# Scoring the samples' cached keys in the even layer instead of in the attention stage

## The chip, the cores and the metric

One core of a Trainium2 chip. The time is device microseconds of one execution of the whole program. Engines: PE (TensorE matmul), PEld (its weight loads), DVE (VectorE), ACT (ScalarE), POOL (GpSimd) and SP (SyncE, which issues most DMAs). Arrays live in device memory (DRAM), working tiles in the on-chip buffer, matmul results in PSUM.

## The reference

One inference step of two layers. The even layer has HGRN2 heads (chunked gated linear attention) and forgetting-attention heads ("fox") side by side; the odd layer is GLA. A prompt of 2048 tokens is worked on together with samples: 8 sequences of 4 new tokens, each with 2048 past tokens in a paged cache. The change touches the samples' attention to that cache:

```
def fox_sample(q, k, v, log_f, k_pages, v_pages, logf_pages, page_table):
    ...
    k_past = k_pages[page_table].reshape(db, -1, H, dh)
    v_past = v_pages[page_table].reshape(db, -1, H, dh)
    lf_past = logf_pages[page_table].reshape(db, -1, H).astype(jnp.float32)
    ...
    suffix_past = (lax.cumsum(lf_past, axis=1, reverse=True) - lf_past).swapaxes(1, 2)
    logit_past = jnp.einsum('bthd,bshd->bhts', q, k_past).astype(jnp.float32) * scale \
        + cum_new[..., None] + suffix_past[:, :, None, :]
    ...
    p = jax.nn.softmax(jnp.concatenate([logit_past, logit_new], axis=-1), axis=-1).astype(v.dtype)
    return jnp.einsum('bhts,bshd->bthd', p[..., :P], v_past) + jnp.einsum('bhts,bshd->bthd', p[..., P:], v)
```

There are 8 sequences x 16 pages; a page holds 128 keys x 4 heads x 128 elements in float32, 256 KB. The keys are 32 MB, the values 32 MB.

## The kernel before

The program has four stretches: the even layer's first half of the prompt, its second half (with the samples), the attention stage (`phase_fox`), and the odd layer. A half of the even layer is 16 dense **units** (weights of one projection against all tokens of the half, three float16 matmuls for each product, lines 630 to 632), numbered 0 to 15 and 16 to 31 and given by `staged`; each unit is yielded in pieces, n = 0, 1, 2, 3 and so on. Beside them run four heads of linear attention (`lin_attn`, lines 700 to 930: gl, gd, qA, kA, o_A and the like), woven in by `mux` in proportion to costs written in the code. Between pieces `staged` calls `ahead(pool, u, n)`, which works on the cached keys, and `beside`, which measures the scale of 20 "later" weight units (a load `lr`, four DVE reduces at line 307, a small matmul `spr`); all 20 are in the second half.

**Keys.** One tile is four pages (1 MB): one page column j of four sequences (group g = 0 or 1), 32 tiles in all. A loaded tile (`kp` or `pgcache_fox_k`) is turned by four DVE transposes (`turn_block`, line 1535) into `kt`, keys along the free dimension. 20 of the tiles (`AHEAD`, units 4 to 13 and 19 to 28) are loaded at piece 1 (line 1531), turned at piece 3 and piece 0 of the next unit, and stored at line 1551 to the DRAM array `kT`. They use buffers "lr" in the first half and "wr" in the second, where raw weights are loaded too.

**Attention.** `fox_prompt` (scores `s`, softmax through `mx`, `nm` and `L`, transposes `pt`, their float16 parts `th` and `tl`, products with the values `fo`) and `fox_sample` are generators; `until` steps the one that is behind by the costs they yield, scaled by `FOX_P` and `FOX_S`. `fox_sample` first makes `qz` (queries masked for a sequence, line 1630). Then for each tile n it fetches the turned tile `ktd` from `kT` (line 1597), or loads four pages and turns them into `kts`, and gives the 16 matmuls of the tile before (`score`, line 1697) through `strips`: four heads side by side on 32 columns of PE each, into a PSUM bank `sc` of four pages:

```
            return lambda: nc.tensor.matmul(sc[32 * h : 32 * h + 32, j % 4 * P : (j % 4 + 1) * P], qz[:, g, 4 * h + x],
                                            kt[:, 4 * h + x], start=(j % 4, g, x) == (0, 0, 0), stop=False,
```

After four page columns, 16 matmuls of `sel` with `suf` (line 1726) add the forget values' suffix sums of `past()`, and one DVE instruction (line 1729) adds a zero column, takes the maximum and writes the bank to `pr`. After four banks come the exponential, the transposes of `pr` to `pT`, and for each of 32 value tiles a fetch (`pgcache_fox_v`) and four matmuls (`pv`, line 1777).

Three things order this. `issue_after` places an instruction behind a named one in the recorded order. `KAHEAD` and `PKLAG` keep the turning and the scores within a distance of the prompt's work. `page_regs` reads page numbers into SP's registers, so page loads go through SP's queue in order.

Of the kernel before, what the change touches and what calls it, by code (L numbers as in the profile page):

```python
# [8 lines left out]
F32 = mybir.dt.float32  # L9
# [10 lines left out]
P = 128  # L20
# [14 lines left out]
SC_C = 1350.0  # L35
# [4 lines left out]
EWR = 3  # L40
# [10 lines left out]
AHEAD = (*range(4, 14), *range(19, 29))  # L51
PRE = len(AHEAD)
TURNED = [n for n in range(2 * 16) if (n + 1) * PRE // 32 > n * PRE // 32]
PAST = 3
VAHEAD = 3
KAHEAD = 6
PKLAG = 4
# [10 lines left out]
PV_C = 5860.0  # L68
# [60 lines left out]
class Kern:  # L129
# [6 lines left out]
    def consts(self):  # L136
# [31 lines left out]
        self.kT = dp.tile([PRE, P, 4 * 512], F32, name="kT")  # L168
# [465 lines left out]
    def proj_fm(self, pps, act, W, off, M, hf, evac, nm):  # L634
        for c0, n in self.segs(hf):
            ps = pps.tile([P, 512], F32, tag="pj", name=f"pf_{nm}{c0}")
            for k in range(KT):
                self.mm3(ps[:M, :n], [x[:, k, off : off + M] for x in W],
                         [x[:, k, c0 : c0 + n] for x in act], k == 0, k == KT - 1)
# [3 lines left out]
    def proj_tm(self, pps, act, W, hf, evac, nm, width=256, pairs=True, banks=("pj",)):  # L643
# [3 lines left out]
        for g in range(0, len(tl), per):  # L647
# [8 lines left out]
            for j, (c0, n) in enumerate(grp):  # L656
                for k in range(KT):
                    self.mm3(ps[:n, j], [x[:, k, c0 : c0 + n] for x in act],
                             [x[:, k, :width] for x in W], k == 0, k == KT - 1)
# [463 lines left out]
    def phase_even(self):  # L1123
# [4 lines left out]
        with pool("act", side="right") as ap, pool("w", side="right") as w0, pool("wl", side="right") as wp1, \  # L1128
                pool("wk") as wp0, pool("nrm") as n0, pool("stt") as sp, pool("ps", space=PSUM) as pp0:
            wpool = self.wpool = Pool(w0, {"w": 3, "wr": EWR, "rm": 2, "pow": 2, "lr": 2})  # L1130
            wp = Pool(wp0, {"c4": 7, "sam": 1, "v4": 3, "sg": 3, "pd": 1, "kt": 2, "y": EY, "xpad": 1, "vs": 3,
                            "ss": 2, "rs_t": 2, "rs_r": 2}, Pool(wp1, {"c2": EC2, "th": ETH}))
# [14 lines left out]
            def beside(x):  # L1147
                x -= 33
                for n in (1, 2):
                    if 0 <= x - 1 < len(self.later):  # L1150
                        self.later[x - 1][n]()
                if 0 <= x < len(self.later):
                    self.later[x][0]()

            self.later, self.kept = [], {}
# [4 lines left out]
            for hf in range(2):  # L1160
# [7 lines left out]
                def dense(a, b, hf=hf):  # L1168
                    return self.staged(us, 16 * hf + a, 16 * hf + b, beside)
# [33 lines left out]
                else:  # L1203
                    self.sx_odd = self.gain_scale(self.g_odd, pps, "pj", "o")
                    self.later = [self.later_unit(wpool, pps, w, cols, key, undo) for w, cols, key, undo in
                                  self.later_units()]
# [7 lines left out]
                drain(dense(2 - hf, 3))  # L1214
                drain(mux(lin(0), LIN_E[hf], dense(3, 5), 2 * cost))
# [35 lines left out]
            for n in range(2):  # L1251
                self.ahead(wpool, 32, n)
# [14 lines left out]
    def staged(self, us, a, b, beside=None):  # L1267
# [1021 lines left out]
```

## Time and profile before

| | |
|---|---|
| median of 3 runs | 2319.26 us (2313.12 to 2326.04) |
| profiled execution | 2321.78 us, its span 2320.1 us |
| mean granted clock of TensorE | 0.983 |
| even layer, attention, odd layer (about, in the trace) | 0 to 880, 880 to 1260, 1260 to 2320 us |
| stores and fetches of turned keys | 20 and 20, of 1024 KB |
| page loads of keys | 80 of 256 KB in the even layer, 48 in the attention |

In a row of grouped instructions or of the timeline, the line of the kernel, engine and operation come first, then output <- inputs, the shape, how often (x), the busy time and the mean of one in ns, and last the idle time of that engine ahead of them with what ended it. "PE s L630 <- DVE mx L1421: 16.8, 12, 7.5" reads: PE waited before the matmuls into s for DVE's instructions on mx, 16.8 us in all, 12 times, 7.5 us at the longest. PE's granted clock is a share of full speed.

### The profile page before, as it was taken

To read this page: it belongs to the slowest core of one execution; us is meant where nothing else is said; L and a number is where in the kernel's file an instruction comes from. 1 tells how busy PE (TensorE), PEld (TensorE's weight loads), DVE (VectorE), ACT (ScalarE), POOL (GpSimd) and SP (SyncE) were. 2 spreads that over 40 slices of the span, in tenths; PEclk is the share of its full clock that TensorE was granted. 3 is DMA by queue.
4 is the path that set the end of the run, shared out by engine and by line. 5 is a ranking of instruction groups with operands and counts; after the bars stand their busy time and mean duration, and the time that the engine had idled before them with its cause. 6 is when DMAs were issued, how large, how long until landed. Compare 5 with 4: busy or idle time off the path is not lost.

```text
span 2320.1 us, 58035 instructions
## 1 busy us (share of the span) xinstructions
PE 2206.3 (95%) x23316; PEld 1580.6 (68%) x23316; DVE 1399.2 (60%) x3138; ACT 991.6 (43%) x2200; POOL 727.1 (31%) x788
## 2 busy tenths in 40 slices
PE   7999999999999996889999999999999999999998
PEld 5677667864655684556446888677677666667887
DVE  7766567626555555768768445366665655547554
ACT  6433344221121223446566443555544545545343
POOL 2223334001111103434346245154452432323232
PEclk9999999999999998999999999999999999999999
DMA  6356665975766549997984969524224431115553
GB/s 203 121 163 187 192 194 188 284 177 172 224 197 183 169 136 271 250 264 271 277 265 142 311 196 262 126 75 146 73 92 97 126 94 58 47 58 165 169 188 151
DMA packets 365296, 403.87 MB, mean 174 GB/s; under 512 B 108529, under 2 KB 303410, under 8 KB 355810
## 3 DMA queue, kind: packets, MB, share of 16 engines
q1 hardware_dynamic: 362882, 393.54, 57.4%
q0 software_dynamic: 2144, 6.62, 0.8%
q8 instruction: 183, 3.00, 0.5%
q14 instruction: 87, 0.71, 0.1%
HBM read 265.77 MB, written 117.39 MB: 165 GB/s over the span
## 4 chain that ended last, share of the span: by engine, by line
PE 69%; DMA 10%; DVE 8%; ACT 4%; issue 4%; SPq 2%; POOL 2%; POOLq 0%; DVEq 0%; ACTq 0%
PE pt_o L630 4%; PE pt_o L631 4%; PE pt_o L632 4%; DMA pgcache_fox_k<-in_cache_fox_k 3%; PE pt_Cv L630 2%; PE pt_Cv L632 2%; PE pt_Cv L631 2%; PE pt L1457 2%; DMA ny<-in_x_prompt 1%; PE pv L1777 1%; PE gl_A L761 1%; PE o_C L914 1%; PE pt_Av L632 1%; PE pt_Av L630 1%; PE pt_Av L631 1%
## 5 line engine op out<-in xcount | busy, mean ns | idle before, releaser
L630 PE MATMUL pt_o<-w_o,act 128*128 128x256 f16 x1024 | 278.9, 273 | 1.3 <-ACT sg1C L687 1.3
L631 PE MATMUL pt_o<-w_o,act 128*128 128x256 f16 x1024 | 278.9, 273 | 0.0
L632 PE MATMUL pt_o<-w_o,act 128*128 128x256 f16 x1024 | 278.7, 273 | 0.0
L630 PEld LDWEIGHTS <-act 128*128 128x128 f16 x2304 | 226.6, 98 | 37.1 <-issue 3.7
L631 PEld LDWEIGHTS <-act 128*128 128x128 f16 x2304 | 226.7, 98 | 33.5 <-issue 4.8
L632 PEld LDWEIGHTS <-act 128*128 128x128 f16 x2304 | 226.6, 98 | 30.7 <-issue 2.2
L794 POOL TENSOR_TENSOR kA<-kA,fA 128x512 f32<-128x512 f32 (+1 forms) x56 | 76.8, 1372 | 338.8 <-PE gl_A L761 275.7
L1429 ACT ACTIVATE L<-L,nm,kc 128x512 f32<-128x512 f32 (+3 forms) x160 | 118.2, 741 | 75.1 <-DVE nm L1427 58.6
L630 PE MATMUL pt_Cv<-w_Cv,act 128*128 128x256 f16 (+1 forms) x512 | 141.4, 276 | 0.3 <-DMA act<-xs 0.3
L632 PE MATMUL pt_Cv<-w_Cv,act 128*128 128x256 f16 (+1 forms) x512 | 141.3, 276 | 0.0
L631 PE MATMUL pt_Cv<-w_Cv,act 128*128 128x256 f16 (+1 forms) x512 | 141.3, 276 | 0.0
L1437 POOL TENSOR_SCALAR L<-L,nm 128x512 f32<-128x512 f32 (+3 forms) x160 | 100.0, 639 | 130.7 <-DVE nm L1433 65.4
L794 POOL TENSOR_TENSOR kC<-kC,fC 128x512 f32<-128x512 f32 (+1 forms) x56 | 81.9, 1463 | 136.3 <-PE gl_C L761 91.4
L1464 ACT ACTIVATE th<-pt 128x512 f16<-128x512 f32 (+3 forms) x159 | 81.0, 527 | 94.6 <-PE pt L1457 92.7
L1465 DVE TENSOR_TENSOR tl<-pt,th 128x512 f16<-128x512 f32 (+3 forms) x159 | 94.5, 605 | 13.0 <-ACT th L1464 11.2
L1457 PE MATMUL pt<-ident,L 128*128 128x128 f32 x544 | 89.6, 280 | 9.4 <-DVE tl L1465 7.5
L1457 PEld LDWEIGHTS pt<-ident,L 128*128 128x128 f32 x544 | 65.5, 143 | 36.1 <-DVE tl L1465 12.8
L793 DVE TENSOR_TENSOR qC<-qC,fC 128x512 f32<-128x512 f32 (+1 forms) x56 | 72.9, 1301 | 21.1 <-PE gl_C L761 21.1
L1977 ACT ACTIVATE vC<-pt_Cv,kc 128x512 f32<-128x512 f32 (+1 forms) x40 | 23.9, 598 | 133.9 <-PE pt_Cv L632 133.9
L630 PE MATMUL s<-k,q 128*128 128x512 f16 (+3 forms) x160 | 57.4, 359 | 20.0 <-DVE mx L1421 16.8
L630 PE MATMUL pt_Bv<-w_Bv,act 128*128 128x260 f16 (+1 forms) x256 | 70.4, 275 | 3.5 <-DVE kc L279 2.3
L630 PE MATMUL pt_Bk<-w_Bk,act 128*128 128x256 f16 x256 | 71.3, 278 | 0.3 <-DVE Bvs L1075 0.3
(961 smaller groups left out, 6473.9 us busy)
## 6 DMA issues: line engine op xcount, KB each, us to landing
pgcache_fox_v<-in_cache_fox_v SPq DMA_DIRECT2D x128, 256.0 KB, 4.5
kp<-in_cache_fox_k SPq DMA_DIRECT2D x80, 256.0 KB, 5.3
kT<-kt SPq DMA_DIRECT2D x20, 1024.0 KB, 5.0
ktd<-kT SPq DMA_DIRECT2D x20, 1024.0 KB, 14.1
yr<-yT SPq DMA_DIRECT2D x16, 1024.0 KB, 7.3
pgcache_fox_k<-in_cache_fox_k SPq DMA_DIRECT2D x48, 256.0 KB, 13.3
x1d<-xo SPq DMA_DIRECT2D x44, 256.0 KB, 4.2
wr_o<-in_w_out_even SPq DMA_DIRECT2D x32, 256.0 KB, 5.5
```

What stands on the lines that cost most here:

```text
L630: nc.tensor.matmul(ps, lh[0], rh[0], start=first, stop=False)
L631: nc.tensor.matmul(ps, lh[0], rh[1], start=False, stop=False)
L632: return nc.tensor.matmul(ps, lh[1], rh[0], start=False, stop=last)
L761: nc.tensor.matmul(ps[o : o + M, ch], k[:, ch * P + r : ch * P + r + M], rhs[:, :, 1], start=True, stop=True, tile_position=(0, o))
L793: nc.vector.tensor_tensor(xv[:, :, 1], xv[:, :, 1], t0.to_broadcast([P, nb, w]), ALU.mult)
L794: nc.gpsimd.tensor_tensor(kv[:, :, 0], kv[:, :, 0], t1.to_broadcast([P, nb, w]), ALU.mult)
L1429: self.last_exp = nc.scalar.activation(lt[:, :w], lt[:, :w], AF.Exp, bias=nm[:, 0:1], scale=ib, accum_out=nm[:, 2 + j : 3 + j])
L1437: nc.gpsimd.tensor_scalar(lt[:, :w], lt[:, :w], nm[:, 1:2], 2.0**14, ALU.mult, ALU.mult)
L1457: nc.tensor.transpose(pt[:, w : w + P], rows[b][s // 4][0][:, (s % 4) * P : (s % 4 + 1) * P], self.ident)
L1464: nc.scalar.activation(th[:, a:w], pt[:, a:w], AF.Copy),
L1465: nc.vector.tensor_tensor(tl[:, a:w], pt[:, a:w], th[:, a:w], ALU.subtract)))
L1977: r = nc.scalar.activation(v[h][:, g : g + cnt], ps[:, :, :256], AF.Copy, scale=c)
```

## The change

All 32 key tiles are handled in the even layer, at positions t = 4 x unit + piece that the list `KEYS` gives: four at 52, 56, 60 and 64, then one at every second t from 68 to 122. A tile is loaded at t, turned at t + 2 and t + 3, and its 16 matmuls are given at t + 4, behind the last dense matmul given so far, into a bank of "gr", the two banks that the linear attention's gl and gd use. For g = 0 ACT copies the result to `scs`, for g = 1 DVE adds its result to that, and at t + 5 the 64 KB are stored to the DRAM array `scd`. `kT` goes. `qz` is made at unit 12 (`queries`). Ten later units move into the first half. The attention fetches the scores as one 1 MB load into `pr`, and adds them where it took the maximum; its yields are longer in places, so that the sample's work is spread over the prompt's in another way. Buffers: "wr" 4 in place of 3, "lr" 1 in place of 2, "rm" and "pow" 3 in place of 2.

```
-EWR = 3
+EWR = 4
-AHEAD = (*range(4, 14), *range(19, 29))
+KEYS = (*range(4 * 13, 4 * 17, 4), *range(4 * 17, 4 * 31, 2))
+LATER = (*range(4, 14), *range(17, 27))
-PV_C = 5860.0
+PV_C = 10080.0
...
-        self.kT = dp.tile([PRE, P, 4 * 512], F32, name="kT")
+        self.scd = dp.tile([P, T], F32, name="scd")
...
-            wpool = self.wpool = Pool(w0, {"w": 3, "wr": EWR, "rm": 2, "pow": 2, "lr": 2})
+            wpool = self.wpool = Pool(w0, {"w": 3, "wr": EWR, "rm": 3, "pow": 3, "lr": 1})
...
+            def beside(j, n):
+                if n == 0 and j - 1 in LATER:
+                    for step in self.later[LATER.index(j - 1)][1:]:
+                        step()
+                if n == 1 and j in LATER:
+                    self.later[LATER.index(j)][0]()
...
+                if beside and n < 4:
+                    self.ahead(self.wpool, pps, 4 * j + n)
+                    beside(j, n)
...
-                with ExitStack() as st:
-                    if len(self.pks) > PKLAG:
-                        st.enter_context(self.tc.issue_after(self.pks[-1 - PKLAG].ins))
-                    self.last_pe = self.mm3(ps[:, :w], q, [x[:, :w] for x in K[h, j]], True, True)
+                self.last_pe = self.mm3(ps[:, :w], q, [x[:, :w] for x in K[h, j]], True, True)
...
+    def queries(self, wp, s):
+        nc = self.nc
+        if s == 0:
+            self.q4 = wp.tile([P, 512], F32, tag="c2", name="q4").rearrange("p (x t) -> p x t", t=TS)
...
+            return
+        with self.tc.issue_after(self.last_dve.ins):
+            for hp in range(2):
+                x = slice(8 * hp, 8 * hp + 8)
+                for g in range(2):
+                    nc.vector.scalar_tensor_tensor(self.qz[:, g, x], self.q4[:, x], self.fsc["q", hp][1],
+                                                   self.bm[:, g : g + 1].to_broadcast([P, 8, TS]), ALU.mult, ALU.mult)
+
+    def ahead(self, pool, pps, t):
+        nc, wp = self.nc, self.few
+        if t in (4 * 12, 4 * 12 + 2):
+            self.queries(wp, t % 4)
+
+        def turns(x):
+            with self.tc.issue_after(self.last_dve.ins):
+                self.made += [self.turn_block(self.kt_ahead, self.kp_ahead, y) for y in (x, x + 1)]
+
+        if t - 5 in KEYS and KEYS.index(t - 5) % 2:
+            j = KEYS.index(t - 5) // 2
+            nc.sync.dma_start(self.scd[:, j * P : (j + 1) * P], self.scs)
+        if t - 4 in KEYS:
+            j, g = divmod(KEYS.index(t - 4), 2)
+            ps = pps.tile([P, 512], F32, tag="gr", name=f"ks{j}{g}")[:, :P]
+            kt, made = self.kts.pop(0)
+
+            def score(x, h):
+                return lambda: nc.tensor.matmul(ps[32 * h : 32 * h + 32], self.qz[:, g, 4 * h + x], kt[:, 4 * h + x],
+                                                start=x == 0, stop=x == 3, tile_position=(0, 32 * h))
+
+            with self.tc.issue_after(self.last_mm.ins):
+                self.strips([score(x, h) for x in range(4) for h in range(NH)], made)
+            if g == 0:
+                self.scs = wp.tile([P, P], F32, tag="scs", name=f"scs{j}")
+                nc.scalar.activation(self.scs, ps, AF.Copy)
+            else:
+                nc.vector.tensor_tensor(self.scs, ps, self.scs, ALU.add)
+        if t - 3 in KEYS:
+            turns(2)
+            self.kts.append((self.kt_ahead, self.made))
+        if t - 2 in KEYS:
+            n = KEYS.index(t - 2)
+            self.kt_ahead, self.made = pool.tile([P, NH * 4, P], F32, tag="wr", name=f"kt{n}"), []
+            self.kp_ahead = self.kps.pop(0)
+            turns(0)
+        if t in KEYS:
+            n = KEYS.index(t)
+            kp = pool.tile([P, 4, 512], F32, tag="wr", name=f"kp{n}")
             with self.tc.issue_after(self.last_sp.ins):
-                regs = self.page_regs(TURNED[m] % 2, TURNED[m] // 2)
+                regs = self.page_regs(n % 2, n // 2)
                 for x in range(4):
-                    self.page_load(self.kp_ahead, "cache_fox_k", regs[x], x)
...
+                    self.page_load(kp, "cache_fox_k", regs[x], x)
+            self.kps.append(kp)
...
+        nc.sync.dma_start(pr[:, :T], self.scd)
+        yield 8000
...
+        for c in range(4):
+            sc = pps.tile([P, 512], F32, tag="sc", name=f"sc{c}")
+            for jj in range(4):
+                for h in range(NH):
+                    nc.tensor.matmul(sc[32 * h : 32 * h + 32, jj * P : (jj + 1) * P],
+                                     env["sel"][:, 4 * c + jj].rearrange("p b t -> p (b t)"), env["suf"][:, h],
+                                     start=jj == 0, stop=jj == 3, tile_position=(0, 32 * h))
+            part = pr[:, c * 512 : (c + 1) * 512]
+            nc.vector.tensor_tensor_reduce(part, sc, part, 1.0, -3e38 if c == 0 else mx[:, c - 1 : c], ALU.add, ALU.max,
+                                           mx[:, c : c + 1])
+            yield 3000
```

In the rows of order that follow, a number behind a name tells its buffer; ISA is the prompt's add with a running maximum, and its read of that maximum.

On DVE at the attention's start, in the first head's second group, before:

```order
L1535 STREAM_TRANSPOSE kts00_11760<-pgcache_fox_k00_11755 128x16x32
L1421 ISA L070_11769,mx07_11764<-s070_11765,cb0_11493 128x512
L1421 ISA mx07_11764 128x1
L1535 STREAM_TRANSPOSE kts00_11760<-pgcache_fox_k00_11755 128x16x32 x3
L1480 SCALAR_TENSOR_TENSOR fy000_11791<-fo00_11566,kc_67,fsg00_11496 128x512
L1432 TENSOR_REDUCE nm06_11675<-nm06_11675 128x1
L1421 ISA L071_11776,mx07_11764<-s071_11772,cb0_11493,mx07_11764 128x384
L1421 ISA mx07_11764 128x1
L1535 STREAM_TRANSPOSE kts01_11948<-pgcache_fox_k01_11943 128x16x32 x3
```

and after:

```order
L1418 TENSOR_SCALAR nm06_12846<-mx06_12832,kc_67 128x1
L1412 ISA L070_12879,mx07_12874<-s070_12875,cb0_12664 128x512
L1412 ISA mx07_12874 128x1
L1456 TENSOR_TENSOR tl0003_12824<-pt0003_12821,th0003_12823 128x128
L1412 ISA L071_12885,mx07_12874<-s071_12881,cb0_12664,mx07_12874 128x384
L1412 ISA mx07_12874 128x1
L1412 ISA L071_12885,mx07_12874<-s071_12881,cm07_12872,mx07_12874 128x128
L1412 ISA mx07_12874 128x1
L1471 SCALAR_TENSOR_TENSOR fy000_12899<-fo00_12737,kc_67,fsg00_12667 128x512
```

The transposes between the parts of row block 7's maximum are gone, and with them the waits for pages that stood ahead of it.

On PE in the second half, within the unit Bk0 (output pt_Bk100), before:

```order
L632 MATMUL pt_Bk100_10249<-w_Bk01_9635,act_121 128x256
L630 LDWEIGHTS act_121
L630 MATMUL pt_Bk100_10249<-w_Bk01_9635,act_121 128x256
L631 LDWEIGHTS act_121
L631 MATMUL pt_Bk100_10249<-w_Bk01_9635,act_121 128x256
```

and after:

```order
L627 MATMUL pt_Bk100_11031<-w_Bk01_10249,act_121 128x256
L1571 MATMUL ks110_10647<-kt22_10446,qz_4856 32x128 x16
L625 LDWEIGHTS act_121
L625 MATMUL pt_Bk100_11031<-w_Bk01_10249,act_121 128x256
L626 LDWEIGHTS act_121
L626 MATMUL pt_Bk100_11031<-w_Bk01_10249,act_121 128x256
```

The 16 score matmuls of key tile 22 now stand between two of the unit's dense matmuls, and those behind them pass only when they have.

On DVE in the second half, where the linear attention of head 1 ends (y_A111) and that of head 2 begins (qA12), before:

```order
L744 SCALAR_TENSOR_TENSOR y_A1110_8952<-py_A1110_8947,g_hgrn_781,sg11_6896 128x512
L1535 STREAM_TRANSPOSE kt14_8900<-kp14_8751 128x16x32
L1535 STREAM_TRANSPOSE kt15_9129<-kp15_9014 128x16x32 x3
L296 TENSOR_REDUCE pow_Cg3_9141<-spr_Cg3_9139 128x1
L1535 STREAM_TRANSPOSE kt15_9129<-kp15_9014 128x16x32
L307 TENSOR_REDUCE rm_o11_9550<-lr_o11_9335 128x1 x4
```

and after:

```order
L739 SCALAR_TENSOR_TENSOR y_A1110_9436<-py_A1110_9431,g_hgrn_781,sg11_6921 128x512
L1526 STREAM_TRANSPOSE kt17_9489<-kp17_9328 128x16x32 x4
L291 TENSOR_REDUCE pow_o11_9837<-spr_o11_9835 128x1
L280 TENSOR_SCALAR pow_o11_9837<-pow_o11_9837 128x1
L281 TENSOR_SCALAR kc_67<-pow_o11_9837 128x1
L1526 STREAM_TRANSPOSE kt18_9626<-kp18_9492 128x16x32 x4
L282 RECIPROCAL kc_67<-kc_67 128x1
L1580 TENSOR_TENSOR scs8_9487<-ks81_9608,scs8_9487 128x128
L1526 STREAM_TRANSPOSE kt19_9784<-kp19_9629 128x16x32 x4
L702 COPY_PREDICATED dg_882<-mdiag_861,gd_A12_9700 128x256
```

Twelve transposes of three key tiles now stand together where five stood, with the four reduces of a later weight unit gone from there.

More of the change, by code (lines that the diff above doesn't have):

```diff
@@ L34 @@
 S0 = 12000.0
-SC_C = 1350.0
 Z_C = 4000.0
@@ L1214, in phase_even @@
                 drain(dense(2 - hf, 3))
+                if hf == 0:
+                    self.sx_odd = self.gain_scale(self.g_odd, pps, "pj", "o")
+                    self.later = [self.later_unit(wpool, pps, w, cols, key, undo) for w, cols, key, undo in
+                                  self.later_units()]
                 drain(mux(lin(0), LIN_E[hf], dense(3, 5), 2 * cost))
@@ L1250, in phase_even @@
             drain(last)
-            for n in range(2):
-                self.ahead(wpool, 32, n)
+            for t in range(4 * 32, 4 * 32 + 2):
+                self.ahead(wpool, pps, t)
     def later_units(self):
@@ L1589, in pages @@
             return t, r
-        def turned(n):
-            kt = fs.tile([P, NH * 4, P], F32, tag="pg", name=f"ktd{n}")
-            with ExitStack() as st:
-                if len(asked) < 8:
-                    st.enter_context(self.tc.issue_after(first_v.ins))
-                d = nc.sync.dma_start(kt.rearrange("p a s -> p (a s)"), self.kT[n])
-            asked.extend([d] * 4)
-            kts.append((kt, [d]))
         yield S0
-        marks, steps, first_v = [], [], self.last_vload
+        marks, first_v = [], self.last_vload
         qs = one([P, NH, TS], "qs")
@@ L1690, in past @@
                                  start=False, stop=True)
[L1691 removed]
+                yield 2000
             suf = one([P, NH, P], "suf")
             nc.vector.tensor_copy(suf, psf)
[L1694 to L1699 removed]
@@ L1701, in fox_sample @@
-        kts, ins = [], []
-        sc = None
-        for n in range(2 * NPG + 1):
-            if n < 2 * NPG:
-                j, g = n // 2, n % 2
-                if n in TURNED:
-                    turned(TURNED.index(n))
-                    yield 4 * SC_C
-                else:
-                    yield from turn(pages("cache_fox_k", g, j)[0], g, j)
-            if n == PAST:
-                yield from past()
-                self.y_bounds(pps)
-            if n == 0:
-                continue
-            j, g = (n - 1) // 2, (n - 1) % 2
-            c = j // 4
-            if (j % 4, g) == (0, 0):
-                sc = pps.tile([P, 512], F32, tag="sc", name=f"sc{c}")
-            kt, made = kts.pop(0)
-            self.pks.append(self.strips([score(h, g, j, x, kt, sc) for x in range(4) for h in range(NH)],
-                                        made))
-            if (j % 4, g) == (3, 1):
-                for jj in range(4):
-                    for h in range(NH):
-                        nc.tensor.matmul(sc[32 * h : 32 * h + 32, jj * P : (jj + 1) * P],
-                                         env["sel"][:, 4 * c + jj].rearrange("p b t -> p (b t)"), env["suf"][:, h],
-                                         start=False, stop=jj == 3, tile_position=(0, 32 * h))
-                nc.vector.tensor_tensor_reduce(pr[:, c * 512 : (c + 1) * 512], sc, env["zcol"].to_broadcast([P, 512]), 1.0,
-                                               -3e38 if c == 0 else mx[:, c - 1 : c], ALU.add, ALU.max,
-                                               mx[:, c : c + 1])
-                yield 1200
@@ new lines, in past @@
+            env.update(suf=suf, sel=sel, mnew=mnew, ntb=ntb)
+        yield from past()
+        self.y_bounds(pps)
+        for c in range(4):
[9 more added lines that the diff above has]
+            yield 3000
```

99 lines of the change are left out of this document (20 added, 79 removed).

## The prediction

> **What bounds the kernel now.** I read the page first, then busy time by stage, then the waits of the attention stage.
>
> ```profile
> span 2320.1 us, 58035 instructions
> PE 2206.3 (95%) x23316; PEld 1580.6 (68%) x23316; DVE 1399.2 (60%) x3138; ACT 991.6 (43%) x2200; POOL 727.1 (31%) x788
> PE   7999999999999996889999999999999999999998
> PE 69%; DMA 10%; DVE 8%; ACT 4%; issue 4%; SPq 2%; POOL 2%; POOLq 0%; DVEq 0%; ACTq 0%
> ```
>
> PE is busy 95% of the span and nearly everywhere, except in three slices just past the middle (6, 8, 8). Moving work of PE's from one full stage to another gains nothing; only PE's idle time and its slow clock can go. The busy table by stage says where they are (columns: length, busy time and count of PE, PEld, DVE, ACT, POOL, then PE's granted clock, the DMA engines' share, GB/s). The rows are the even layer's first half, its second half, the attention's first 200 us, the attention's rest, and the odd layer:
>
> ```profile
> 0.00:440.00 440.00, 411.23 (x4681) 302.99 (x4682) 298.90 (x678) 186.15 (x425) 132.24 (x138) 0.99 0.61 184
> 440.00:880.00 440.00, 428.25 (x4454) 288.55 (x4451) 234.27 (x533) 92.06 (x231) 53.52 (x56) 0.99 0.65 190
> 880.00:1080.00 200.00, 162.45 (x1822) 104.29 (x1822) 139.52 (x463) 91.01 (x221) 68.75 (x132) 0.91 1.04 268
> 1080.00:1260.00 180.00, 171.54 (x1137) 91.67 (x1138) 137.56 (x449) 112.31 (x267) 84.72 (x138) 0.99 0.70 222
> 1260.00:2320.00 1060.00, 1032.83 (x11228) 793.12 (x11225) 588.94 (x1018) 510.06 (x1057) 387.90 (x326) 0.99 0.45 138
> ```
>
> The attention's first 200 us lose 200 − 162.45 = 37.6 us idle, and (1 − 0.91) × 200 = 18 us to the clock, while the DMA engines are full (1.04). It is the stretch in which the cached keys are fetched, turned and scored. Its rest, with the values in place of the keys, loses 8.5 us idle and 1% of clock. The even layer's second half, which is to take the work over, has PE busy 428 of 440 us: no room on PE, much on DVE (234 of 440).
>
> What PE and DVE waited for in the attention (total, times, longest), and one such wait by the clock:
>
> ```profile
> DVE kts L1535 <- DMA pgcache_fox_k<-in_cache_fox_k: 26.3, 7, 11.0
> PE s L630 <- DVE mx L1421: 16.8, 12, 7.5
> PE pt L1457 <- DVE tl L1465: 7.5, 7, 3.7
> PE sc L1697 <- DMA ktd<-kT: 6.1, 2, 4.6
> PE fo L631 <- DVE tl L1465: 5.4, 7, 2.3
> PE s L630 <- DMA vn<-vs: 3.0, 1, 3.0
> 910.05 1.90 DVE L1535 STREAM_TRANSPOSE kts<-pgcache_fox_k 128x512 f32<-128x512 f32 x3 [7.41 <-DMA pgcache_fox_k<-in_cache_fox_k]
> 912.31 0.61 PE L630 MATMUL s<-k,q 128*128 128x512 f16 x1 [7.54 <-DVE mx L1421]
> ```
>
> By name PE waits for the prompt's own softmax (mx, tl). The last two rows show what stands behind that name: at 910.05 DVE had stood 7.41 us before a transpose whose page had not landed, the prompt's maximum was queued behind it, and PE's 7.54 us ended 2.3 us later. A wait of DVE for a page becomes a wait of PE for mx.
>
> **What goes from the attention.** First the scores' matmuls:
>
> ```profile
> L1697 PE MATMUL sc<-ktd,qz x640: 272/273/422, 903.2 to 1063.3; 128*32 128x128 f32 x160
> L1697 PE MATMUL sc<-kts,qz x384: 272/273/423, 901.5 to 1061.5; 128*32 128x128 f32 x192
> 942.31 1.08 PE L1697 MATMUL sc<-ktd,qz 128*32 128x128 f32 x32
> 943.32 0.49 PE L1688 MATMUL psf<-stri,lfTs 128*128 128x128 f32 x2
> 1051.62 2.76 PE sc L1697 x96
> ```
>
> 640 + 384 = 1024 records are 32 tiles of 32 records (16 program matmuls, two passes each). They overlap, so a tile's price is the time until the next matmul starts: 943.32 − 942.31 = 1.01 us for a tile that stands alone, 2.76 / 3 = 0.92 us in threes (from the chain of waits). Middle 0.97: 32 × 0.97 = **−31 us**. The 16 sel matmuls of each bank stay.
>
> Then the waits. Of 37.6 + 18 = 55.6 us I let 16 stay: what remains of the stretch, about 200 − 31 − 40 = 129 us, loses at the rate of the attention's rest, 8.5 / 180 idle and 1% clock, 7.4 us; the rest is a wait that has nothing to do with keys (vn, 3.0) and the start's own softmax chain. So **−40 us**. Bounds: −50 (5 or 6 stay) and −17 (rival B). What speaks for the high end: the queue that made DVE wait empties. These fetches leave it:
>
> ```profile
> ktd<-kT SPq DMA_DIRECT2D x20, 1024.0 KB, 14.1
> kT<-kt SPq DMA_DIRECT2D x20, 1024.0 KB, 5.0
> pgcache_fox_k<-in_cache_fox_k SPq DMA_DIRECT2D x48, 256.0 KB, 13.3
> ```
>
> 20 MB of turned keys and 12 MB of raw ones no longer arrive during attention, and 20 MB are no longer stored before it. What comes instead is one fetch of the 1 MB of scores, and 16 stores of 64 KB in the even layer, under 2 MB together. The values' 32 MB now start near the attention's beginning, since the sample's yields are longer, so its traffic is spread rather than front-loaded.
>
> **What the even layer takes over.** The same 512 matmuls, now in a dense stream that leaves no gap: **+31 us** (29 at 0.92, 32 at 1.01). They stand alone there, 16 between dense ones, so the upper price is the nearer, but the price in threes is the lower end.
>
> [...]
>
> DVE's part is in the next rows (groups of the first half's and then the second half's transposes, a reduce of the second half, and a 128x128 copy of the attention):
>
> ```profile
> L1535 DVE STREAM_TRANSPOSE kt<-kp 128x512 f32<-128x512 f32 x40 | 25.8, 684 | 9.2 <-DMA kp<-in_cache_fox_k 9.2
> L1535 DVE STREAM_TRANSPOSE kt<-kp 128x512 f32<-128x512 f32 x40 | 25.9, 685 | 9.8 <-DMA kp<-in_cache_fox_k 9.7
> L307 DVE TENSOR_REDUCE rm_o<-lr_o 128x1 f32<-128x512 f32 x32 | 20.0, 674 | 3.7 <-DMA lr_o<-in_w_out_even 3.7
> L1755 DVE COPY pT<-ppt 128x128 f32<-128x128 f32 x16 | 3.4, 277 | 0.3 <-PE ppt L1752 0.3
> ```
>
> Three of the 32 tiles are turned in the first half and 29 in the second. The first half loses 28 of 40 transposes (19 us) and gains 10 later units of 4 reduces (27 us): DVE 299 to about 307 of 440. The second half gains 76 transposes (52 us), loses 40 reduces (27 us), and gains 16 adds of 0.28 us (by the copy's row): 234 to about 264 of some 485. Both lie under PE, so their busy time costs nothing; the 16 ACT copies (ACT 92 of 440) neither. The qz products and their small loads move from the attention's start into unit 12; DVE has slack there too. If the cover failed where a DVE burst meets the linear attention's chain (12 transposes within three adjacent pieces, 8 us), PE would wait for that chain; that is in the next term.
>
> What costs is **new waits of PE**. In before nothing on PE in the even layer needed a turned key; now every tile's 16 matmuls stand in PE's order, with the whole dense stream behind them, and need four transposes which need four page loads issued two pieces ahead, as before. What such a wait does, by two places of the trace:
>
> ```profile
> DVE kt L1535 <- DMA kp<-in_cache_fox_k: 18.9, 5, 8.0
> 786.41 1.90 DVE L1535 STREAM_TRANSPOSE kt<-kp 128x512 f32<-128x512 f32 x3 [8.00 <-DMA kp<-in_cache_fox_k]
> 789.30 1.06 PE L761 MATMUL gl_A<-qA,kA 128*32 128x16 f32 x64 [4.09 <-DVE qA L793]
> 788.40:795.00 6.60, 5.70 (x87) 4.33 (x88) 5.55 (x11) 0.95 (x2) 1.50 (x1) 0.50 0.51 191
> 603.90 0.79 PE L914 MATMUL o_A<-Sx,qA 128*128 128x128 f32 x2 [1.55 <-DVE Sx L920]
> 602.00:604.00 2.00, 0.45 (x3) 0.26 (x3) 2.00 (x5) 0.00 (x0) 0.00 (x0) 0.98 0.38 131
> 604.00:607.40 3.40, 3.40 (x12) 2.31 (x13) 3.40 (x9) 2.24 (x11) 0.00 (x0) 0.51 0.00 0
> ```
>
> Of 20 tiles five waited for their pages, 18.9 us on DVE. The longest, 8.0 us, cost PE 4.09 us idle and then 6.6 us at clock 0.50, 3.3 us lost: 7.4 in all. By that share all five cost at most 18.9 / 8.0 × 7.4 = 17.5 us for 20 tiles, 0.87 a tile; 12 more tiles give 10.5. For the scores' own waits on transposes, and on a PSUM bank that the linear attention now shares with them, I add half as much, 5.5: together **+16 us**. Bounds: 0 (every tile's transposes end before PE comes to it; most have some 5 us or more by the order) and +53 (rival A); it is nearest to the rows of before, which show one tile in four waiting but only some reaching PE.
>
> [...]
>
> **Sum.** −31 − 40 + 31 + 16 = **−24 us**. Against the profiled execution's 2321.8 us (span 2320.1) that is 2298; the median shown lies 2.5 us lower, so 2295 against it; I state 2297.
>
> **Rivals.**
> A, slower: the second half's waits get worse than they were. One tile in four of its 29 waits for its pages as at 786, but with PE itself behind it: 7 × 7.4 = 53 us in place of 16, −31 − 40 + 31 + 53 = +13, **2335**. For it: weights' loads, page loads and more buffers of "wr" share SP's queue, and keys follow each other every half unit instead of every unit. Against: 20 MB of stores leave the even layer, and the lead between load and transpose is the same. It decides from 40 us of waits, five or six such tiles, and makes the kernel slower by over 0.5% from 52 us, seven.
>
> B, no change: the attention's idle time is its own softmax chain, as the names say. Then 16.8 + 7.5 + 5.4 = 29.7 us idle and half of the clock's 18 stay; −17 in place of −40: −31 − 17 + 31 + 16 = −1, **2320**. Against it: the rows at 910 and 912, and that the attention's rest runs the same chain with PE at 95%. For it: DVE stays the second busiest there (137.56 of 180).
>
> C, better: no new wait in the even layer, and 50 us of waits go: −31 − 50 + 31 = −50, **2270**. For it: the slack in the order; against: one tile in four of before's waited.
>
> That the change might not take effect I leave out: the order shows no transpose and no key left in the attention, which is all that B could rest on otherwise.
>
> **How the numbers follow.** Forecast 0.50, A 0.17, B 0.18, C 0.15. About 0.5% (11.6 us) is what a measurement can tell from no change. Faster by more: forecast 0.46, C 0.15, the good side of B 0.05: 0.66. Within: 0.04 + 0.04 of A + 0.13 of B: 0.21. Slower: 0.13, all A. The range reaches to C's time (2273) and to about half way between B's and A's (2326), leaving some 0.08 below and 0.10 above.
>
> **What would show it.** Right: the attention some 70 us shorter, its first part with DMA share well under 1, clock near 0.99, and PE over 93% busy; the even layer's second half some 45 us longer, 31 of them in the scores' matmuls. Wrong by A: rows of PE's scores waiting for transposes, of DVE waiting for kp, over 40 us in all, with clock under 0.95 in the second half. Wrong by B: PE still waiting 20 us or more for mx and tl in the attention, with no DVE wait for a DMA before it. Wrong by C: the second half longer by only the matmuls.

## The result, and the profile after

Four runs of the kernel after gave a median of 2289.4 us (2286.85 to 2291.65), against 2319.45 us (2313.12 to 2326.04, four runs): ratio 0.987, 95% interval 0.984 to 0.990. It is about 30 us faster; 2297 was forecast, in a range of 2273 to 2326. One execution of the experiment with fetches made but unused took 3730 us at a granted clock of 0.56 and does not count in its ratio; every other run below is undisturbed.

The page of the kernel after (span; engines; PE by slices; PE's clock; the DMA queue that carries nearly all traffic):

```profile
span 2289.9 us, 58071 instructions
PE 2195.9 (96%) x23316; PEld 1569.0 (69%) x23316; DVE 1400.7 (61%) x3154; ACT 994.3 (43%) x2216; POOL 724.9 (32%) x787
PE   7999999999999999899999999999999999999998
PEclk9999999999999999999999999999999999999999
q1 hardware_dynamic: 359570, 353.69, 52.7%
```

The dip of three slices has shrunk to one. PE's busy total fell only from 2206.3 to 2195.9: the work is the same, and the gain is idle time and clock. The stages, by busy time. The even layer's last dense matmul now starts at 911.2 (879.6 before) and the output projection at 1239.0 (1268.5 before), so the rows are the even layer's halves, the attention in two parts, and the odd layer:

```profile
0.00:440.00 440.00, 408.51 (x4681) 299.13 (x4682) 314.27 (x755) 185.42 (x424) 136.16 (x146) 0.99 0.55 170
440.00:911.00 471.00, 461.27 (x5476) 313.60 (x5474) 253.72 (x524) 96.70 (x248) 49.10 (x46) 1.00 0.66 170
911.00:1060.00 149.00, 134.94 (x954) 74.91 (x952) 116.91 (x433) 91.03 (x222) 72.25 (x138) 0.98 0.83 257
1060.00:1239.00 179.00, 166.75 (x1069) 96.40 (x1067) 138.47 (x439) 118.42 (x284) 90.77 (x143) 0.96 0.51 152
1239.00:2289.90 1050.90, 1024.46 (x11148) 784.97 (x11145) 577.32 (x1005) 502.70 (x1039) 376.59 (x315) 0.99 0.45 136
```

For comparison, before, cut at the same events:

```profile
440.00:879.40 439.40, 427.78 (x4452) 288.37 (x4450) 234.18 (x532) 92.06 (x231) 53.52 (x56) 0.99 0.65 190
879.40:1080.00 200.60, 162.92 (x1827) 104.47 (x1824) 139.61 (x463) 91.01 (x221) 68.75 (x132) 0.91 1.04 268
1080.00:1268.50 188.50, 180.04 (x1217) 99.57 (x1218) 143.67 (x459) 118.07 (x277) 90.19 (x143) 0.99 0.70 221
1268.50:2320.10 1051.60, 1024.33 (x11149) 785.22 (x11146) 582.82 (x1009) 504.30 (x1048) 382.43 (x321) 0.99 0.45 137
```

| stage | before | after | forecast | measured |
|---|---|---|---|---|
| even layer | 879.4 | 911.0 | +47 | +31.6 |
| attention | 389.1 | 328.0 | −71 | −61.1 |
| odd layer | 1051.6 | 1050.9 | 0 | −0.7 |
| span | 2320.1 | 2289.9 | −24 | −30.2 |

In the attention PE's idle time fell from 389.1 − 162.92 − 180.04 = 46.1 to 328.0 − 134.94 − 166.75 = 26.3 us, and what its clock lost from 0.09 x 200.6 + 0.01 x 188.5 = 19.9 to 0.02 x 149 + 0.04 x 179 = 10.1: together 30 us. The other 31 us are the size of the scores' matmuls. The even layer is longer by just those matmuls: its idle time is 440 − 408.51 + 471 − 461.27 = 41.2 us, against 440 − 411.23 + 439.4 − 427.78 = 40.4.

PE's waits in the attention after, DVE's longest item of the even layer, and PE's waits before the scores' matmuls there:

```profile
PE s L625 <- DVE mx L1412: 7.4, 12, 2.6
PE pt L1448 <- DVE tl L1456: 5.6, 8, 1.6
PE fo L625 <- ACT th L1455: 3.5, 5, 1.6
PE s L625 <- DVE Bvs L1070: 3.0, 1, 3.0
DVE kt L1526 <- DMA kp<-in_cache_fox_k: 39.7, 11, 18.8
PE ks L1571 <- DVE scs L1580: 3.0, 1, 3.0
PE ks L1571 <- DVE kt L1526: 1.0, 2, 0.6
```

The wait for mx is 7.4 us in place of 16.8, and the long single ones (7.5) are gone. DVE's wait for key pages in the even layer has doubled (39.7 in place of 18.9 us), and yet PE shows next to none of it: before `ks` it waited 4.0 us in all. So much is read from two traces. Which part of the change earned the 61 us, and what the even layer really pays, the experiments had to say.

### The profile page after: what moved, and what is told of

It is laid out like the page before. It is cut to its first block, busy times and chain, and to the rows that moved or that the text cites. A ratio compares the mean times of both kernels' runs of the same rounds, so it can differ in the third digit from the quotient of the medians.

```text
span 2289.9 us, 58071 instructions
## 1 busy us (share of the span) xinstructions
PE 2195.9 (96%) x23316; PEld 1569.0 (69%) x23316; DVE 1400.7 (61%) x3154; ACT 994.3 (43%) x2216; POOL 724.9 (32%) x787
## 4 chain that ended last, share of the span: by engine, by line
PE 42%; DVE 3%; ACT 2%; DMA 2%; POOL 2%; issue 1%; SPq 0%; POOLq 0%; DVEq 0%; ACTq 0%
PE pt_o L625 4%; PE pt_o L626 4%; PE pt_o L627 4%; PE pt_Cv L625 2%; PE pt_Cv L627 2%; PE pt_Cv L626 2%; PE o_C L909 1%; PE gl_C L756 1%; PE pt L1448 1%; POOL s_C L842 1%; PE py_C L728 1%; ACT L L1420 1%; DMA wr_o<-in_w_out_odd 1%; PE fo L626 0%; PE fo L627 0%
## 5 line engine op out<-in xcount | busy, mean ns | idle before, releaser
L1526 DVE STREAM_TRANSPOSE kt<-kp 128x512 f32<-128x512 f32 x128 | 82.1, 684 | 40.7 <-DMA kp<-in_cache_fox_k 39.7
L1448 PEld LDWEIGHTS pt<-ident,L 128*128 128x128 f32 x544 | 65.8, 143 | 39.1 <-DVE tl L1456 10.1
L363 POOL TENSOR_TENSOR w_o<-wr_o,w_o 128x512 f16<-128x512 f32 x32 | 46.5, 1467 | 79.1 <-ACT w_o L362 55.2
```

The costliest lines, as they stand in the source:

```text
L363: nc.gpsimd.tensor_tensor(lo, r, hi, ALU.subtract)
L1448: nc.tensor.transpose(pt[:, w : w + P], rows[b][s // 4][0][:, (s % 4) * P : (s % 4 + 1) * P], self.ident)
L1526: return self.nc.vector.transpose(kt[:, :, 32 * x : 32 * x + 32], t[:, x].rearrange("p (a e) -> p a e", e=32))
```

## The experiments

All times are medians, and ratios are against before, which ran beside each group of experiments on the same chip: 2320.9 us beside the two experiments with a quarter of the scores, no turning and no key traffic; 2321.3 beside turning only, slower keys, unused fetches and PV_C 11100; 2322.2 beside the other four. The kernel after was not run again beside them, so differences of some 3 us from its 2289.4 are not told apart. The even layer, which no edit to the kernel before touches, ends between 876 and 887 us in the traces of its variants: that is the scatter of a single trace.

### What the even layer pays

**A quarter of the scores**, in the kernel after:

```
-                                                start=x == 0, stop=x == 3, tile_position=(0, 32 * h))
+                                                start=True, stop=True, tile_position=(0, 32 * h))
...
-                self.strips([score(x, h) for x in range(4) for h in range(NH)], made)
+                self.strips([score(0, h) for h in range(NH)], made)
```

> The kernel after, with 4 of each key tile's 16 score matmuls (three quarters of the products of the cached keys are left out; loads, transposes, evictions, stores and the rest stay). Theory: the matmuls are the whole price of the work taken over, PE waits for next to nothing else; three quarters of 31 us go from the even layer, 2289 -> about 2266, the even layer ends near 888 instead of 911, the attention stays at 328 us. [...] Rival 2 (the even layer is bound by DVE's waits for pages): under 10 us.

Measured: 2275.2 us, ratio 0.978 (0.976 to 0.981); 14 us under the kernel after's 2289.4. That misses the expected 23, and by its size could mean a fixed price per tile. The trace decides otherwise. The even layer ended at 891, 20 us earlier, and the attention took 328 us as before; the odd layer was 3.7 us longer in this trace (1054.6), which nothing in the edit explains. A tile's price, in the kernel after and then in this one (start, busy, engine, line, instruction; the next row is what follows it on PE):

```profile
882.26 1.08 PE L1571 MATMUL ks<-kt,qz 128*32 128x128 f32 x32
883.27 0.28 PE L627 MATMUL pt_Bk<-w_Bk,act 128*128 128x256 f16 x1
```

```profile
864.02 0.43 PE L1571 MATMUL ks<-kt,qz 128*32 128x128 f32 x8
864.38 0.28 PE L627 MATMUL pt_Bk<-w_Bk,act 128*128 128x256 f16 x1
```

883.27 − 882.26 = 1.01 us for 16 matmuls, 0.36 for 4: 32 x 0.65 = 21 us, which is the stage's 20. By these two points 12 matmuls are worth 0.65 us and a tile's fixed part is an estimated 0.36 − 4 x 0.65 / 12 = 0.14 us, under 5 us for all 32. The full price is 32 x 1.01 = 32 us, the whole of the even layer's 31.6. A waiting time of 16 us beside it isn't there.

**No turning**, in the kernel after: the matmuls read the loaded pages as they lie.

```
         if t - 3 in KEYS:
-            turns(2)
             self.kts.append((self.kt_ahead, self.made))
...
-            self.kp_ahead = self.kps.pop(0)
-            turns(0)
+            kp, self.made = self.kps.pop(0)
+            self.kt_ahead = kp.rearrange("p x s -> p (x s)").rearrange("p (a s) -> p a s", s=P)
```

> The kernel after, with the score matmuls reading the loaded pages as they are: no transposes and no turned tile (the scores are of unturned keys). 128 transposes, 82 us of DVE, and DVE's 39.7 us of waits for pages leave DVE; PE itself then waits for the pages, where it must, one position later than DVE did. Theory: both are covered by PE, so the time stays within 0.4% (2280 to 2294). Rival (what DVE does late is paid by PE through the linear attention and the evictions): 10 to 20 us less, 2270 to 2279, with PE's idle time in the even layer down from 41 us by as much.

Measured: 2286.5 us, ratio 0.983 (0.981 to 0.985), 3 us under the kernel after and within the expected 0.4%; the rival (2270 to 2279) fell. The edit also leaves the turned tiles' buffers free. The even layer's second half in this run:

```profile
440.00:909.30 469.30, 463.57 (x5475) 313.92 (x5473) 186.04 (x399) 97.17 (x248) 50.66 (x46) 1.00 0.66 170
```

DVE is busy 186 in place of 254 us, and the stage is 1.7 us shorter. Transposes and DVE's waits for pages are covered by PE nearly in full.

**Buffers undone**: 3 of "wr" and 2 of "lr".

```
-EWR = 4
+EWR = 3
...
-            ... "pow": 3, "lr": 1})
+            ... "pow": 3, "lr": 2})
```

> The kernel after with one part undone: 3 buffers of wr and 2 of lr, in place of 4 and 1. Loads of key pages and of raw weights, and the turned tiles, then share 3 buffers. Theory (arrivals and transposes in the even layer are covered by PE, as the run without turning showed): 2285 to 2300. Rival (with a buffer less the page loads start so late that PE comes to the score matmuls before the transposes): 2305 or more, with PE's waits before ks from 4 us to over 20.

Measured: 2296.6 us (2294.3 to 2300.8), ratio 0.9905 (0.988 to 0.993): some 7 us slower than the kernel after. Its even layer ends at 919.4, and its waits there are:

```profile
PE ks L1571 <- DVE kt L1526: 4.4, 3, 3.5
DVE kt L1526 <- DMA kp<-in_cache_fox_k: 62.5, 13, 18.8
```

DVE waits 62.5 us in place of 39.7, and PE waits 4.4 for the transposes in place of 1.0, far from the rival's 20; the median lies in the expected range. The rest of the 8 us has no one name. The cover has an edge, and the buffers as the change sets them keep the kernel clear of it.

### What the attention gains

**A quarter of the scores, in the kernel before**: fetches, loads and transposes stay.

```
-            self.pks.append(self.strips([score(h, g, j, x, kt, sc) for x in range(4) for h in range(NH)],
+            self.pks.append(self.strips([score(h, g, j, 0, kt, sc) for h in range(NH)],
```

> The kernel before, with 4 of each key tile's 16 score matmuls in the attention (three quarters of those products left out; fetches, loads and transposes stay). Theory: the matmuls cost 0.97 us a tile there, so three quarters of 31 are 23 us, less what falls into stretches where PE waited for pages anyway: 2296 to 2308. Rival (the attention's first part was bound by the pages, so that matmuls were free in it): within 6 us of before, 2313 or more.

Measured: 2317.2 us (2307.6 to 2326.7, ten runs), ratio 0.9974 (0.995 to 0.9997): 4 us (by the interval 1 to 11), where the products by themselves are 20 or more. The theory (2296 to 2308) fell and the rival came true. The trace is of the slowest of the ten; its even layer ends 8 us later than before's, and its attention takes 386.9 us in place of 389.1. The attention's first part in it, from 887:

```profile
887.00:1080.00 193.00, 141.24 (x1042) 77.87 (x1040) 138.38 (x460) 87.00 (x210) 68.83 (x131) 0.89 1.05 272
```

PE does 141 us of work in place of 163, the DMA engines are as full as before (1.05), and PE's idle time has grown from 38 to 52 us: what the matmuls leave becomes waiting. In the kernel before, PE did not bind this stretch.

**No key traffic, in the kernel before**: one constant resident tile (zeros) stands in for every key tile of the attention; nothing is fetched, loaded or turned there, and all matmuls stay. **Turning only** puts the 48 transposes back, on a resident tile; its edit is the two shown under "Which traffic", together.

```
+        kt0 = fs.tile([P, NH * 4, P], F32, tag="pg", name="kt0")
+        set0 = nc.gpsimd.memset(kt0, 0.0)
...
-                if n in TURNED:
-                    turned(TURNED.index(n))
-                    yield 4 * SC_C
-                else:
-                    yield from turn(pages("cache_fox_k", g, j)[0], g, j)
+                kts.append((kt0, [set0]))
+                for x in range(4):
+                    yield SC_C
```

> The kernel before, with the attention's key tiles replaced by one resident tile: no fetch of a turned tile, no load of a raw one and no transpose in the attention (the scores are of constant keys there); all 512 score matmuls and the whole even layer stay. Theory: 30 us of the attention's 61 us are waits for this traffic, and go: 2319 -> about 2290, PE's idle time in the attention from 46 to under 25 us. Rival 1 (the waits are the prompt's own softmax chain): 2310 or more. Rival 2 (the matmuls themselves made the gaps, by standing ahead of the prompt's): 2305 or more.

> The kernel before, with resident tiles in the attention in place of every fetch of a turned tile and every load of a raw one; the 48 transposes (33 us of DVE) and all 512 matmuls stay, on constant keys. The run without any key traffic gave 2281, of which this puts the transposes back. Theory (the attention's first half waits for arrivals, DVE in order with the pages and PE with the turned tiles): the transposes alone are covered, 2278 to 2291. Rival (33 us of DVE work within the prompt's chain of maxima are what PE waited for): 2300 or more.

Measured: 2280.9 us without all of it, ratio 0.981 (0.979 to 0.984), and 2290.9 with the transposes, ratio 0.988 (0.984 to 0.992). Both theories held, the first with more than its 30 us, and the rivals (2300, 2305 or 2310 and more) fell. The attention took 347.7 and 356.8 us in these traces. So the traffic, with the waiting for it, is worth 30 us at least, with every matmul still made. Whether the other 10 are the transposes stays open: the run with turned tiles only, below, has the same 48 transposes and comes to 2280.4. The first of the two is faster than the kernel after: in an attention that isn't held up the scores cost some 20 us (347.7 − 328.0; the two attentions differ in pace too), in the dense stream of the even layer 31.6.

**Slower keys**: other costs for the interleaving alone.

```
-SC_C = 1350.0
+SC_C = 1700.0
...
-PV_C = 5860.0
+PV_C = 5000.0
```

> The kernel before with other costs alone: a key tile's quarter counts 1700 in place of 1350, a value tile 5000 in place of 5860, so that the keys are asked for over a quarter more of the prompt's work and the values over less, and the sample ends about 4% later. Nothing else differs. Theory (arrivals are late because 32 MB are asked for in 160 us at a DMA share of 1.04): the waits shrink, 2300 to 2314. Rival (each tile's latency, not the rate, sets the wait): within 5 us of 2321. If the pace were the whole of the gain, 2290.

Measured: 2314.9 us (2305.9 to 2319.2, ten runs), ratio 0.997 (0.9947 to 0.9995). This other pace is worth 6 us (by the interval 1 to 12), just outside what was expected (2300 to 2314) and more than the rival's 5; it is not the change's 30. It is the only other pace tried in the kernel before; the kernel after's was not.

**Fetches made but unused**: all fetches and page loads of the attention stay; nothing is turned, nothing waits for them, the matmuls read one constant tile.

```
-            kts.append((kt, [d]))
+            kts.append((kt0, [set0]))
...
-                    yield from turn(pages("cache_fox_k", g, j)[0], g, j)
+                    pages("cache_fox_k", g, j)
+                    kts.append((kt0, [set0]))
+                    for x in range(4):
+                        yield SC_C
```

> The kernel before, with all 20 fetches and 48 page loads of the attention still made, into the same buffers, but nothing waits for them: no transpose, and the matmuls read one resident tile (constant keys). Theory (waiting in order for arrivals): like the run without key traffic, 2278 to 2292. Rival (contention: 32 MB in 160 us with the DMA engines full hold up the prompt's own loads and stores): 2300 or more. In between: both, in that proportion between 2281 and 2321.

Measured: 2322.1 us (nine of ten executions between 2310.1 and 2328.0), ratio 0.999 (0.997 to 1.002): no gain at all. The theory, that the loss is the waiting for arrivals, fell; the rival, contention, came true. PE's first waits in this run's attention:

```profile
PE s L630 <- DMA q<-qd: 13.5, 2, 8.1
PE sc L1697 <- issue: 11.1, 4, 4.3
```

With no one waiting for keys, PE waits for the prompt's own queries instead, a wait that before doesn't show. The run to set beside this one is the one without any key traffic, since neither has transposes or waits for keys, and the scores' matmuls run ahead in both (their last start at 991 and 971 us, before's at 1063). From 900 to 940 and from there to 1060, first with the unused fetches and then without:

```profile
900.00:940.00 40.00, 35.00 (x565) 26.00 (x558) 25.48 (x103) 18.94 (x50) 21.88 (x47) 1.00 1.08 287
940.00:1060.00 120.00, 91.35 (x988) 59.15 (x987) 60.42 (x213) 49.13 (x116) 31.41 (x57) 0.89 1.06 263
900.00:940.00 40.00, 36.39 (x519) 26.44 (x519) 27.31 (x105) 18.84 (x48) 20.69 (x45) 1.00 0.59 202
940.00:1060.00 120.00, 116.02 (x1214) 73.98 (x1215) 89.29 (x320) 75.27 (x182) 51.33 (x92) 1.00 0.36 105
```

Between the two lie 41 us (2322.1 and 2280.9), and the loads of the prompt's queries `q` land in 8.1 us with the traffic and in 3.6 without. The traffic holds the stage up though no one waits for it.

**Which traffic.** Raw pages only: the 20 fetches of turned tiles go, a resident tile stands in. Turned tiles only: the 48 loads of raw pages go, their transposes read a resident tile.

```
-                    turned(TURNED.index(n))
+                    kts.append((kt0, [set0]))
```

```
-                    yield from turn(pages("cache_fox_k", g, j)[0], g, j)
+                    yield from turn(kp0, g, j)
```

> The kernel before with its 20 fetches of turned tiles (20 MB) left out of the attention; one resident tile stands in for them. The 12 raw tiles are still loaded, turned and waited for, and all matmuls stay. All key traffic together was worth 30 us (2321 to 2291 with the transposes kept). Theory (the amount of traffic binds): 20 of the 32 MB go, 30 x 20 / 32 = 19 us: 2296 to 2308. Rival (DVE's standing before raw pages, with the prompt's maxima queued behind it, is what costs): those waits stay, 2312 or more.

> The kernel before with its 48 raw page loads (12 MB) left out of the attention; their transposes read one resident tile and stay. The 20 turned tiles are fetched and waited for, and all matmuls stay. Theory (the amount of traffic binds): 30 x 12 / 32 = 11 us: 2304 to 2314. Rival (DVE's standing before raw pages): 2290 to 2300, since those waits are gone.

Measured: with raw pages only 2313.3 us, ratio 0.996 (0.994 to 0.9985); with turned tiles only 2280.4 us, ratio 0.984 (0.981 to 0.987). Both were to lie by amount of data, 19 and 11 us under before; they lie 9 and 42 under it, both outside what was expected. The first is where the rival, DVE's standing before raw pages, had put it (2312 or more), and the second is below the rival's 2290. But in the run with raw pages only DVE's waits for pages are down from 26.3 to 7.2 us, and most of the time stays. The 20 MB of turned tiles cost nothing once the 12 MB of raw pages are gone. (That run is even 10 us under turning only, which moves less; 4 of them lie in the even layer, which neither edit touches, and the rest has no cause shown.) Why, the DMA queue's row shows, in the same 160 us (900 to 1060) of four runs. Its columns are packets, MB, and the time the packets took as a share of the 16 engines; the rows after it, where there are any, are fetches with their size and median time to landing.

Before:

```profile
q1 hardware_dynamic: 24283, 41.71, 104.2%
ktd<-kT SPq DMA_DIRECT2D x19, 1024.0 KB, 14.6
pgcache_fox_k<-in_cache_fox_k SPq DMA_DIRECT2D x44, 256.0 KB, 14.3
```

Turning only, without any of the two:

```profile
q1 hardware_dynamic: 17277, 15.49, 32.7%
```

Raw pages only:

```profile
q1 hardware_dynamic: 24685, 27.07, 69.6%
pgcache_fox_k<-in_cache_fox_k SPq DMA_DIRECT2D x44, 256.0 KB, 7.0
```

Turned tiles only:

```profile
q1 hardware_dynamic: 21723, 37.09, 70.4%
ktd<-kT SPq DMA_DIRECT2D x18, 1024.0 KB, 6.9
```

Raw pages add 27.07 − 15.49 = 11.6 MB and (0.696 − 0.327) x 160 = 59 us of all engines: 196 GB/s. Turned tiles, and the values that start a little sooner, add 21.6 MB in 60 us: 358 GB/s. A byte of a raw page thus takes 1.8 times the engines' time. Together they fill the engines (104%) and land late, a page of 256 KB after 14 us and a turned tile after 15; either alone leaves some 30%, and lands in 7. With turned tiles alone PE is hardly held up; with raw pages alone it is, at the stage's start, where the prefetch asks for several tiles at once: 24 page loads are issued from 900 to 940, where before has 16. From 900 to 940 and from there to 1060, in before, with turned tiles only and with raw pages only:

```profile
900.00:940.00 40.00, 27.17 (x303) 18.37 (x301) 20.44 (x62) 12.73 (x32) 16.08 (x37) 0.74 1.07 285
940.00:1060.00 120.00, 103.38 (x1234) 67.01 (x1232) 87.89 (x288) 55.09 (x133) 37.92 (x68) 0.94 1.08 268
900.00:940.00 40.00, 37.38 (x480) 25.01 (x472) 34.61 (x116) 21.45 (x53) 23.74 (x50) 0.98 0.84 311
940.00:1060.00 120.00, 117.41 (x1378) 76.36 (x1377) 102.10 (x346) 72.60 (x174) 50.19 (x88) 1.00 0.71 226
900.00:940.00 40.00, 25.27 (x262) 16.78 (x264) 21.83 (x64) 10.64 (x27) 14.46 (x35) 0.74 1.09 234
940.00:1060.00 120.00, 112.99 (x1469) 75.80 (x1462) 98.63 (x320) 66.03 (x159) 46.58 (x82) 0.99 0.62 165
```

With raw pages only, the first 40 us have the DMA engines full (1.09) and lose 15 us of PE and a quarter of its clock; the other 120 have room, and lose 7.

The size of the packets does not set raw pages apart: a page of values moves in packets of the same 2 KB, and in before's trace from 1080 to 1240, with values fetched and no keys, such a packet took 84 ns in the median and 98 in the mean. In the trace of the kernel after from 440 to 911, where 123 page loads of keys (128 packets each, 15744 in all) stand among others, 17800 packets of 2 KB took 152 ns in the median and 140 in the mean; with the other 2056 at 98, one of the keys' took an estimated 145 ns. What sets raw pages apart in the code is their place (and the order in which a page's rows are read): `page_load` puts a page of keys on 32 partitions, and a page of values, as large, on all 128. No run here put the key pages on other partitions or read their rows in another order, so what makes it 196 GB/s in place of 358 is not shown.

### Later values

Two runs of the kernel after with PV_C 11100 and 12000 in place of 10080.

> The kernel after with PV_C 11100 in place of 10080: the values' products are spread so that the sample ends about 8% later. In the profile of after, the sample's products end at 1194 and PE is 37% idle and at 0.7 to 0.8 of its clock around 1210 to 1230, with only the prompt's chain left. Theory: sample work fills that gap, 2289 -> 2280 to 2286. Rival: the prompt's last block ends the stage whatever stands beside it, or the sample's own tail then ends last: 2288 or more.

> The kernel after with PV_C 12000 in place of 10080 (11100 gave 2286.4): the sample's work is spread to the prompt's very end. Theory (the gap at the end is filled by 11100 already, and more only moves the sample's tail behind the prompt): 2284 to 2292. Rival (the more spread, the better): under 2283.

Measured: 2286.4 us (2285.4 to 2292.5) and 2301.1 us (2295.6 to 2309.2), ratios 0.987 (0.983 to 0.991) and 0.993 (0.990 to 0.996). The attention's first and last 39 us in the kernel after, and then its last 34 with PV_C 11100:

```profile
911.00:950.00 39.00, 26.06 (x137) 13.19 (x135) 27.38 (x113) 21.54 (x56) 24.71 (x55) 0.91 1.06 307
...
1200.00:1239.00 39.00, 34.04 (x231) 24.91 (x230) 31.12 (x78) 29.47 (x66) 29.02 (x32) 0.87 0.23 69
```

```profile
1200.00:1233.60 33.60, 28.84 (x223) 21.38 (x222) 26.95 (x68) 22.40 (x46) 20.18 (x24) 1.00 0.14 44
```

With 11100 the slow clock at the end (0.87) is gone and the attention is 7 us shorter in that trace (1233.6 − 912.8 = 320.8), but the medians differ by 3 us and their runs overlap: not told apart from the kernel after. With 12000 the attention ends as early (1234.0), and the sample's tail falls into the odd layer, whose first projection waits for it:

```profile
PE pt_o L625 <- ACT act L1853: 6.6, 1, 6.6
PE pt_o L625 <- ACT act L1850: 2.6, 1, 2.6
```

That is worse than both the theory (2284 to 2292) and the rival had it, and a limit on spreading.

## Why the prediction was right, and where it was not

**Its outcome.** −24 forecast, −30 measured, in the range and on the side that held most of the chance. Two terms erred and partly made up for each other, which is luck: the waits that stay in the attention (+10) and the new ones in the even layer (−16). Of its own signs of being right the attention came 61 us shorter instead of some 70, and its first part has PE 134.94 / 149 = 91% busy instead of over 93%; the sign that it named for rival C, a second half longer by only the matmuls, is what happened.

**"−31 for the scores in the attention".** The duration was about right: 0.97 us a tile forecast, and 1.01 in the even layer, where it could be read off again. As a gain of its own it failed: with the traffic in place, leaving out three quarters of the products gave 4 us. PE's work is only worth its time where PE binds, and the prediction's own row (DMA share 1.04, PE idle a fifth of the time) said that it did not there. It is part of the 61 us because the traffic went too. In order: the key traffic with its transposes 389.1 − 347.7 = 41, and then about 20 for the matmuls and all that the two attentions still differ in.

**"−40 for the waits".** Without the key traffic and its transposes before gained 40. In the change itself idle time and clock fell by 30, and 36 us of the whole attention stay rather than some 26 (the forecast's 16 of the first 200 us, and the 10 that the rest lost before): by the rest's rate the prediction let 7 stay, and did not see that the start (26.06 of its 39 us busy, in the last rows above) and the end (0.87 of clock) keep theirs. The mechanism behind the term, DVE standing in order before a page with the prompt's maxima behind it, is in the trace, but taking it away does not bring the time: with no one waiting for a page the time was the same (2322.1 us). What has to go is the traffic of raw pages, which together with the turned tiles fills the DMA engines (104% from 900 to 1060, 70% without the raw pages). That the waits cost nothing beside the traffic is not shown.

**"+31 in the even layer".** Right: 31.6 for the stage, 1.01 us for a tile. The upper price, that of a lone tile, was the one to take.

**"+16 for new waits".** Mis-sized: about 0. PE's idle time in the even layer is as before (41.2 and 40.4 us), and DVE's waits for pages stayed on DVE. The scaling from before's stalls was wrong in kind: it took a wait of DVE for a wait of PE, at 7.4 us for 8.0, though only the one place at 786 had shown that (the rows' other place, at 603.9, has 1.55 us of idle on PE and then 3.4 us at a clock of 0.51). The scores' own waits, put at 5.5, were 4.0. What the other parts of the change do by themselves (ten later units moved to the first half, the values spread further) no run shows; together they leave the even layer and the odd layer where the matmuls alone would put them.

**The rivals.** A did not happen; it came no nearer than the run with the buffers undone, whose even layer is 8 us longer. B fell: the wait for mx shrank from 16.8 to 7.4 us. C's first half (no new wait) came true, its second (50 us of waits go) did not. Two slips bear on none of this: A's 7 x 7.4 is 52 rather than 53, and C's time stands once as 2270 and once as 2273.

## What to carry to other kernels

Before counting work taken off an engine as a gain, see whether that engine binds the stretch: leaving the work out where it stands, with the rest unchanged, showed 4 us in place of some 20. Traffic that no one waited for cost as much here as traffic that was waited for (2322.1 us, and 2321.3 for before beside it), with the DMA engines full (1.06 to 1.08); and a megabyte wasn't a unit of it, since a raw page's cost 1.8 times a turned tile's. A wait on an engine that is covered can double, 18.9 to 39.7 us here, without the bound engine's noticing (PE idle for 40.4 and 41.2 us in the even layer).

## What the runs showed of the hardware that was not expected

The engines' time per byte: 196 GB/s for page loads to 32 partitions, 358 GB/s for tiles to 128, in the same stage; and packets of one size, 2 KB, that took 98 ns in the mean for values and an estimated 145 ns for keys.
